# Turning a feed-forward's relu chunks to channels on VectorE and the transfer queue instead of TensorE

## The chip, the cores and the metric

The kernel runs on one core of a Trainium2 chip. The metric is device time in microseconds (us) of one execution. Engines are named as in the profile: PE is TensorE's matrix multiplication, PEld its weight loads, DVE is VectorE, ACT is ScalarE, POOL is GpSimd, SP is the SyncE queue that issues most transfers.

## The reference, cut to what matters

One decoder layer on 256 tokens of 2048 channels: a token mixer (pooling, gated spatial mixing, sparse attention, merged and projected), then a squared-relu feed-forward of width 8192. The part that the change touches is the feed-forward, with its surroundings:

```
h = rms_norm(x, norm_g[l, 2]) * (1.0 + scale2) + shift2
f = jnp.square(jax.nn.relu(h @ w_ff1[l])) @ w_ff2[l]
x = x + gate2 * rms_norm(f, norm_g[l, 3])
```

All inputs are float32. `w_ff1` is 2048 x 8192 and `w_ff2` 8192 x 2048.

## The kernel before, in words

Every product is made from three matmuls in the type fp32r: activation and weight are each split into a high part and a low part, and high x high, high x low and low x high are summed (lines 188 to 190). The activation is the stationary operand, with channels on the 128 partitions (`hhi`, `hlo` for the first feed-forward product, `fhi`, `flo` for the second); the weight streams, 512 columns at a time. The result therefore comes out with tokens on the partitions, and has to be turned before it can be the activation of the next product.

One `gemm` makes 512 output columns for both token tiles from 16 slices of 128 input channels (`kt`). It has four units. Each unit loads 1 MB of weights into one of three `raw` buffers (line 165, on SP), splits it in two halves (`whi` on ACT, line 175; `wlo` on DVE, line 176; three buffers each), and multiplies: 12 matmuls for each half. So a gemm is 96 matmuls. What waits in the list `later` is issued behind the first unit of the next gemm.

The feed-forward runs in four quarters (`qt`). In each, four gemms over `ff1` (m = 0 to 3) make 512 hidden channels each, and then four gemms over `ff2` (n = 0 to 3) multiply the quarter's 2048 hidden channels and add to `fsum`. Behind each `ff1` gemm, ACT takes the relu of the two PSUM banks into `r_t` (line 945), tokens on partitions. `to_channels` then turns the chunk: eight 128x128 transposes on PE into the two `x` banks (`transposed`, line 345), squares on ACT from PSUM (line 936), and the split into `fhi` (ACT, line 398) and `flo` (DVE, line 399). `to_channels` of chunk m fills slices 4m to 4m+3 of `fhi` and `flo`. The second feed-forward product reads them in rising order, so those of m = 3 are first read three quarters into the gemm n = 0.

During the first two quarters a 1 MB block of `w_adaT` is loaded once a gemm into the same `raw` ring (line 262) and reduced on DVE (line 263).

Each engine's queue runs in order. The order is written before the run by the framework's planner: an instruction takes its place at the time at which the planner believes its operands ready, and among ready ones the earlier in the program goes first; the splits are moved ahead by 150 places (`ahead=150`). Semaphores then make each instruction wait for its real operands. Transfers of a queue share eight completion counters in turn.

Of the kernel before, what the change touches and what calls it, by code (L numbers as in the profile page):

```python
# [7 lines left out]
F32 = mybir.dt.float32  # L8
F32R = mybir.dt.float32r
AF = mybir.ActivationFunctionType  # L10
# [3 lines left out]
P = 128  # L14
# [3 lines left out]
NT = S // P  # L18
# [38 lines left out]
def trunk_kernel(ctx: ExitStack, tc: tile.TileContext, consts, vecs, w_adaT, win_e, win_g, win_n, brp_v, brg_v, brn_v,  # L57
                 wout_v, ff1_v, ff2_v, x, c, pool_w, gmlp_ln_g,
                 gmlp_ln_b, gmlp_ws, gmlp_bs, cmp_w1, cmp_w2, cmp_b2, out):
    nc = tc.nc  # L60
    V, A, T, G = nc.vector, nc.scalar, nc.tensor, nc.gpsimd

    def sbuf(name, side="left", stack=None):
        es = ExitStack()
        p = es.enter_context(tc.tile_pool(name=name, bufs=1, side=side, reuse_waits="tile"))
        (stack or ctx).push(es)
        return p, es
# [17 lines left out]
    def flat(t):  # L85
        return t.rearrange("p j s -> p (j s)")

    def bank(tag):
        return psum["pool"].tile([P, 512], F32, name=f"ps_{tag}", tag=tag, bufs=psum["bufs"][tag])
# [120 lines left out]
    def drain(name):  # L210
        while side[name][0]:
            step(side[name][0])


    later = []

    def gemm(wv, c0, act, k_tiles=KT, row0=0):

        ps = [mm_bank(), mm_bank()]
        for u in range(0, k_tiles, 4):  # L220
            raw = load_raw(wv[c0, (row0 + u) // 4])
            for h in range(2):
                k0 = u + 2 * h
                hv, lv = split(raw[:, 2 * h:2 * h + 2])
                mm_a(ps, k0, k0 == 0, k0 + 2 == k_tiles, act, hv, lv)
            while later:
                later.pop(0)()
            fill()
        return ps

    def gemm_a_last(wv, c0, act, stores, row0=0, between=None, after=()):


        ps = [mm_bank(), mm_bank()]
        kept = []
        for u in range(0, KT, 4):
            raw = load_raw(wv[c0, (row0 + u) // 4])
            for h in range(2):
                k0 = u + 2 * h
                left = (KT - k0) // 2  # L240
                own = left <= len(stores) + 3
                with ExitStack() as es:
                    if k0 >= 4:
                        for ins in after:
                            es.enter_context(tc.issue_after(ins.ins))
                    hv, lv = split(raw[:, 2 * h:2 * h + 2],
                                   stores[len(stores) + 3 - left] if 3 < left and own else None)
                mm_a(ps, k0, k0 == 0, left == 1, act, hv, lv, toks=(0,) if own else range(NT))
                if own:
                    kept.append((k0, hv, lv))  # L250
        if between:
            between(ps)
        for k0, hv, lv in kept:
            mm_a(ps, k0, k0 == 0, k0 + 2 == KT, act, hv, lv, toks=(1,))
        return ps
# [84 lines left out]
    def transposed(src, k2):  # L340

        tb = bank("x")
        for k in range(2):
            for t in range(NT):
                T.transpose(tb[:, (k * NT + t) * P:(k * NT + t + 1) * P],  # L345
                            src[t][:, (k2 * 2 + k) * P:(k2 * 2 + k + 1) * P], ident)
        return tb
# [49 lines left out]
    def hi_lo(hi, lo, src):  # L397
        A.activation(hi, src, AF.Copy)  # L398
        V.tensor_sub(lo, src, hi.bitcast(F32))  # L399
# [360 lines left out]
    tb = bank("x")  # L760
# [159 lines left out]
    fl, _ = sbuf("ff")  # L920
# [9 lines left out]

    def to_channels(m, r_t):

        for k in range(2):
            tb = transposed([r_t[:, t] for t in range(NT)], k)
            r32 = flat(fl.tile([P, 2, S], F32, name="r32", tag="r32", bufs=3))
            A.activation(r32, tb, AF.Square)
            s = slice(4 * m + 2 * k, 4 * m + 2 * k + 2)
            hi_lo(flat(fhi[:, s]), flat(flo[:, s]), r32)

    for qt in range(4):  # L940
        for m in range(4):
            ps = gemm(ff1_v, qt * 4 + m, act) if qt or m else ps_first
            r_t = fl.tile([P, NT, 512], F32, name="r_t", tag="r_t", bufs=2)
            for t in range(NT):
                A.activation(r_t[:, t], ps[t], AF.Relu)  # L945
            later.append(lambda m=m, r_t=r_t: to_channels(m, r_t))
        if qt == 3:
            drain("ada")
        for n in range(4):
            if qt == 3 and n == 3:  # L950
                ps = gemm_a_last(ff2_v, n, (fhi, flo), [[flat(h[:, 4 * k:4 * k + 4]) for h in act] for k in range(4)],
                                 row0=qt * 16)
            else:
                ps = gemm(ff2_v, n, (fhi, flo), row0=qt * 16)
            ns = slice(n * 512, (n + 1) * 512)
            for t in range(NT):
                if qt == 0:
                    V.tensor_copy(fsum[:, t, ns], ps[t])
                else:
                    V.tensor_add(fsum[:, t, ns], fsum[:, t, ns], ps[t])  # L960
                if qt == 3:
                    jk = xp.tile([P, 512], F32, name="jk", tag="jk", bufs=2)
                    A.activation(jk, fsum[:, t, ns], AF.Square, accum_out=ssq3[:, t, n:n + 1])
                    fg[n, t] = fsum[:, t, ns]
                    if n == 3:
                        fg[n, t] = flat(fl.tile([P, 2, S], F32, name="r32", tag="r32", bufs=3))
                    V.tensor_mul(fg[n, t], fsum[:, t, ns], gg2[:, ns])
# [94 lines left out]
```

## Time and profile before

| | us |
|---|---|
| median of three runs | 1498.44 |
| the three runs | 1493.22, 1498.44, 1505.2 |
| the profiled execution, its own time | 1494.34 |
| its span, first to last instruction | 1492.6 |
| PE busy | 1430.4 (96%) |
| DVE busy | 1038.5 (70%) |
| ACT busy | 819.9 (55%) |

The profiled execution's own time is 1.7 us above its span and 4.1 us below the median of the runs. The feed-forward's gemms run from about 775 us of the span to 1483.8 us; the last 8.8 us are the final normalisation and the stores.

### The profile page before, as it was taken

What the parts mean: (1) busy time and instruction counts of PE and PEld (TensorE: products, weight loads), DVE (VectorE), ACT (ScalarE), POOL (GpSimd) and SP (SyncE); (2) the same over time, 40 slices, a digit from 0 to 9 for tenths busy, and PEclk for the clock granted to TensorE, in tenths of its full rate; (3) what the DMA queues carried; (4) which work ended last, traced back from release to release, by engine and by line L of the source; (5) the groups of instructions that cost most, each with busy time, mean ns of one, the idle gap of its engine ahead of it and who ended that gap; (6) DMA issues with size and microseconds to landing.
All of it is one profiled execution on the core that took longest, in us unless ns stands there. A gap on an engine that the chain in (4) does not pass through costs nothing.

```text
span 1492.6 us, 17091 instructions
## 1 busy us (share of the span) xinstructions
PE 1430.4 (96%) x6504; PEld 1167.9 (78%) x6504; DVE 1038.5 (70%) x1297; ACT 819.9 (55%) x1200; POOL 29.8 (2%) x33
## 2 busy tenths in 40 slices
PE   3999999999999999999999999999999999999997
PEld 2777787788777777787778888888888888888886
DVE  7988887768988887788785566565565555444555
ACT  4566666964678874454574543355434554345442
POOL 0000001002010000000000000000000000000000
PEclk9999999999999999999999999999999999999999
DMA  8989788647767567788845666666675455555553
GB/s 321 370 334 366 297 331 307 243 158 245 258 223 280 198 240 306 283 309 317 308 182 190 225 236 237 240 240 241 224 254 191 175 197 199 197 197 178 189 197 113
DMA packets 54098, 365.47 MB, mean 245 GB/s; under 512 B 6128, under 2 KB 6272, under 8 KB 13824
## 3 DMA queue, kind: packets, MB, share of 16 engines
q1 hardware_dynamic: 52704, 360.14, 66.7%
q0 software_dynamic: 1312, 4.23, 0.9%
q8 instruction: 51, 0.84, 0.2%
q14 instruction: 31, 0.25, 0.0%
HBM read 362.26 MB, written 2.10 MB: 244 GB/s over the span
## 4 chain that ended last, share of the span: by engine, by line
PE 83%; DVE 9%; DMA 4%; ACT 3%; issue 1%; SPq 0%; DVEq 0%; ACTq 0%
PE ps_mm L189 26%; PE ps_mm L190 26%; PE ps_mm L188 25%; DVE wlo L176 3%; DVE raw L263 2%; PE ps_x L345 1%; ACT whi L175 1%; DMA raw<-in_win_g_dram 1%; DMA raw<-in_w_out_dram 1%; PE ps_x L668 1%; DMA x_h<-in_x_dram 1%; PE ps_pv L660 1%; PE ps_pv L659 0%; DMA raw<-in_w_br_pool_dram 0%; DMA raw<-in_w_br_nsa_dram 0%
## 5 line engine op out<-in xcount | busy, mean ns | idle before, releaser
L176 DVE TENSOR_TENSOR wlo<-raw,whi 128x1024 fp32r<-128x1024 f32 x479 | 570.9, 1203 | 359.5 <-ACT whi L175 357.2
L175 ACT ACTIVATE whi<-raw 128x1024 fp32r<-128x1024 f32 x479 | 492.6, 1036 | 494.4 <-PE ps_mm L190 409.1
L189 PE MATMUL ps_mm<-wlo,hhi 128*128 128x512 f32 x1240 | 488.4, 394 | 12.8 <-DVE wlo L176 12.8
L188 PE MATMUL ps_mm<-whi,hhi 128*128 128x512 f32 x1240 | 482.8, 394 | 10.0 <-ACT hhi L317 5.5
L190 PE MATMUL ps_mm<-whi,hlo 128*128 128x512 f32 x1240 | 485.9, 392 | 0.0
L189 PEld LDWEIGHTS ps_mm<-wlo,hhi 128*128 128x128 f32 x1240 | 233.8, 189 | 68.4 <-DVE wlo L176 21.4
L188 PEld LDWEIGHTS ps_mm<-whi,hhi 128*128 128x128 f32 x1240 | 233.2, 188 | 60.4 <-ACT whi L175 6.8
L190 PEld LDWEIGHTS ps_mm<-whi,hlo 128*128 128x128 f32 x1240 | 233.7, 189 | 47.8 <-DVE hlo L318 0.4
L263 DVE CUSTOM_DVE_ANT_0 raw<-raw,sil 128x2048 f32<-128x2048 f32 x96 | 219.9, 2292 | 6.6 <-DMA raw<-in_w_adaT_dram 6.6
L188 PE MATMUL ps_mm<-whi,fhi 128*128 128x512 f32 x496 | 193.3, 390 | 0.0
L190 PE MATMUL ps_mm<-whi,flo 128*128 128x512 f32 x496 | 193.0, 389 | 0.0
L189 PE MATMUL ps_mm<-wlo,fhi 128*128 128x512 f32 x496 | 193.0, 389 | 0.0
L190 PEld LDWEIGHTS ps_mm<-whi,flo 128*128 128x128 f32 x496 | 93.1, 188 | 19.4
L189 PEld LDWEIGHTS ps_mm<-wlo,fhi 128*128 128x128 f32 x496 | 93.1, 188 | 19.3
L188 PEld LDWEIGHTS ps_mm<-whi,fhi 128*128 128x128 f32 x496 | 93.1, 188 | 19.2
L395 ACT ACTIVATE ps_mm<-part 128x512 f32<-128x512 f32 x40 | 23.5, 597 | 10.9 <-DVE part L384 7.9
L641 ACT ACTIVATE e<-e,m 128x128 f32<-128x128 f32 (+1 forms) x64 | 28.2, 443 | 0.7 <-DVE m L638 0.6
L945 ACT ACTIVATE r_t<-ps_mm 128x512 f32<-128x512 f32 x32 | 18.8, 588 | 14.7 <-PE ps_mm L190 14.7
L188 PE MATMUL ps_mm<-whi,qe 128*128 128x512 f32 x64 | 24.8, 392 | 1.0 <-ACT whi L175 1.0
L189 PE MATMUL ps_mm<-wlo,qe 128*128 128x512 f32 x64 | 25.3, 395 | 0.5 <-DVE wlo L176 0.5
L345 PE MATMUL ps_x<-cst,x_h 128*128 128x128 f32 x32 | 6.9, 376 | 19.2 <-DVE x_h L336 16.9
L399 DVE TENSOR_TENSOR flo<-r,fhi 128x512 fp32r<-128x512 f32 x32 | 20.7, 689 | 6.4 <-ACT fhi L398 6.4
(287 smaller groups left out, 1124.2 us busy)
## 6 DMA issues: line engine op xcount, KB each, us to landing
raw<-in_w_ff_dram SPq DMA_DIRECT2D x128, 1024.0 KB, 4.8
raw<-in_w_adaT_dram SPq DMA_DIRECT2D x96, 1024.0 KB, 5.8
raw<-in_win_g_dram SPq DMA_DIRECT2D x32, 1024.0 KB, 5.0
raw<-in_win_e_dram SPq DMA_DIRECT2D x24, 1024.0 KB, 6.0
raw<-in_win_e_dram SPq DMA_DIRECT2D x24, 768.0 KB, 6.1
raw<-in_w_out_dram SPq DMA_DIRECT2D x16, 1024.0 KB, 5.5
raw<-in_w_br_nsa_dram SPq DMA_DIRECT2D x8, 1024.0 KB, 5.9
raw<-in_win_e_dram SPq DMA_DIRECT2D x12, 512.0 KB, 5.9
```

Source lines behind the costliest of these rows:

```text
L175: A.activation(hv, v, AF.Copy)
L176: V.tensor_sub(lv, v, hv.bitcast(F32))
L188: T.matmul(outs[t], ahi[:, kt, ts_], hv[:, k, c0:c0 + n], start=f, stop=False, skip_group_check=True)
L189: T.matmul(outs[t], ahi[:, kt, ts_], lv[:, k, c0:c0 + n], start=False, stop=False, skip_group_check=True)
L190: T.matmul(outs[t], alo[:, kt, ts_], hv[:, k, c0:c0 + n], start=False, stop=l, skip_group_check=True)
L263: V.tensor_tensor_reduce(raw, raw, sil, 0.5, 0.0, ALU.mult, ALU.add, accum_out=col)
L345: T.transpose(tb[:, (k * NT + t) * P:(k * NT + t + 1) * P], src[t][:, (k2 * 2 + k) * P:(k2 * 2 + k + 1) * P], ident)
L395: A.activation(ps, early[e][0][:, b * 512:(b + 1) * 512], AF.Copy)
L399: V.tensor_sub(lo, src, hi.bitcast(F32))
L641: A.activation(e[:, br, 0:L], e[:, br, 0:L], AF.Exp, scale=-1.0, bias=m8[:, hh, br:br + 1], accum_out=s8[:, hh, br:br + 1])
L660: T.matmul(po, v, pl, start=False, stop=lst)
L945: A.activation(r_t[:, t], ps[t], AF.Relu)
```

## The change

The relu chunk is turned in two steps. VectorE transposes each 32x32 block of a token tile in place of its position (two instructions a chunk, into `tr`), with the blocks' columns regrouped so that the block column j stands outside. Then 16 transfers on SP move each of the four partition quarters q of `tr` to partition quarter j of `moved`: each takes 32 partitions, two runs of 512 bytes on each, 32 KB. ACT's square reads `moved` from SBUF instead of PSUM, with the blocks put back in order by its access pattern. `to_channels` is issued right behind the relu and no longer put on `later`. TensorE's eight transposes a chunk fall away.

```
     def to_channels(m, r_t):
+        tr = fl.tile([P, 4, NT, 4, 32], F32, name="tr")
+        for t in range(NT):
+            V.transpose(tr[:, :, t], r_t[:, t].rearrange("p (m j i) -> p j m i", m=4, j=4))
+        moved = fl.tile([P, NT, 4, 4, 32], F32, name="moved", tag="moved", bufs=2)
+        for q in range(4):
+            for j in range(4):
+                nc.sync.dma_start(moved[32 * j:32 * j + 32, :, q].rearrange("p t m i -> p t (m i)"),
+                                  tr[32 * q:32 * q + 32, j].rearrange("p t m i -> p t (m i)"))
+        mv = moved.rearrange("p t q m i -> p m (t q) i")
         for k in range(2):
-            tb = transposed([r_t[:, t] for t in range(NT)], k)
             r32 = flat(fl.tile([P, 2, S], F32, name="r32", tag="r32", bufs=3))
-            A.activation(r32, tb, AF.Square)
+            A.activation(r32.rearrange("p (m c i) -> p m c i", m=2, i=32), mv[:, 2 * k:2 * k + 2], AF.Square)
             s = slice(4 * m + 2 * k, 4 * m + 2 * k + 2)
             hi_lo(flat(fhi[:, s]), flat(flo[:, s]), r32)
...
-            later.append(lambda m=m, r_t=r_t: to_channels(m, r_t))
+            to_channels(m, r_t)
```

## Rows read from the trace of the kernel before

**Rows 1.** The page, part 1: busy time of each engine.
```profile
PE 1430.4 (96%) x6504; PEld 1167.9 (78%) x6504; DVE 1038.5 (70%) x1297; ACT 819.9 (55%) x1200; POOL 29.8 (2%) x33
```

**Rows 2.** Windows: length; PE, PEld, DVE, ACT, POOL busy; clock; DMA share.
```profile
820.66:843.32 22.66, 22.66 (x106) 18.85 (x105) 13.22 (x12) 11.58 (x14) 0.00 (x0) 1.00 0.65 233
...
866.00:975.70 109.70, 109.70 (x490) 90.91 (x489) 65.36 (x60) 45.55 (x46) 0.00 (x0) 1.00 0.69 240
...
1153.40:1176.60 23.20, 23.20 (x108) 19.25 (x107) 12.40 (x12) 12.58 (x16) 0.00 (x0) 1.00 0.52 182
...
1333.10:1355.80 22.70, 22.70 (x106) 18.87 (x105) 11.10 (x10) 11.58 (x14) 0.00 (x0) 1.00 0.53 185
```

**Rows 3.** Timeline of PE, one chunk's boundary and its transposes: start, duration.
```profile
815.21 0.39 PE L188 MATMUL ps_mm<-whi,hhi 128*128 128x512 f32 x1
...
820.43 0.40 PE L190 MATMUL ps_mm<-whi,hlo 128*128 128x512 f32 x1
820.66 1.03 PE L345 MATMUL ps_x<-cst,r_t 128*128 128x128 f32 x8
...
821.77 0.40 PE L189 MATMUL ps_mm<-wlo,hhi 128*128 128x512 f32 x1
```

**Rows 4.** Groups of 128x512 instructions from 785 us to 1483 us.
```profile
L399 DVE TENSOR_TENSOR flo<-r,fhi 128x512 fp32r<-128x512 f32 x32 | 20.7, 689 | 6.4 <-ACT fhi L398 6.4
...
L936 ACT ACTIVATE r<-ps_x 128x512 f32<-128x512 f32 x32 | 17.1, 585 | 0.0
...
L963 ACT ACTIVATE jk<-fsum 128x512 f32<-128x512 f32 x7 | 4.3, 618 | 9.0 <-DVE fsum L960 9.0
```

**Rows 5.** Timeline of ACT around the same boundary, with idle before.
```profile
814.73 0.60 ACT L945 ACTIVATE r_t<-ps_mm 128x512 f32<-128x512 f32 x1 [0.98 <-PE ps_mm L190]
815.41 1.06 ACT L175 ACTIVATE whi<-raw 128x1024 fp32r<-128x1024 f32 x1
816.38 0.58 ACT L945 ACTIVATE r_t<-ps_mm 128x512 f32<-128x512 f32 x1
818.13 1.06 ACT L175 ACTIVATE whi<-raw 128x1024 fp32r<-128x1024 f32 x1 [1.17 <-PE ps_mm L190]
...
832.63 1.06 ACT L175 ACTIVATE whi<-raw 128x1024 fp32r<-128x1024 f32 x1 [1.66 <-PE ps_mm L190]
```

**Rows 6.** Timeline of DVE around the same boundary.
```profile
814.93 2.28 DVE L263 CUSTOM_DVE_ANT_0 raw<-raw,sil 128x2048 f32<-128x2048 f32 x1
...
817.14 1.22 DVE L176 TENSOR_TENSOR wlo<-raw,whi 128x1024 fp32r<-128x1024 f32 x1
```

**Rows 7.** Timeline of SP there: weight loads issued.
```profile
815.04 0.33 SPq L165 DMA_DIRECT2D raw<-in_w_ff_dram  x1
...
817.25 3.56 SPq L165 DMA_DIRECT2D raw<-in_w_ff_dram  x2
```

**Rows 8.** Waits of the SP queue: total us, times, longest.
```profile
SPq L262 <- DMA x_h<-in_x_dram: 2.3, 2, 1.4
...
SPq L165 <- DMA sil<-in_c_dram: 0.7, 1, 0.7
```

**Rows 9.** Timeline of SP: issues of single transfers, first and last of the kernel.
```profile
1.18 0.42 SPq L129 DMA_DIRECT2D sil<-in_c_dram  x1
...
1488.80 0.33 SPq L974 DMA_DIRECT2D out_dram<-x  x1
```

**Rows 10.** DMA issues: count, size, median us from issue to landing.
```profile
raw<-in_w_ff_dram SPq DMA_DIRECT2D x128, 1024.0 KB, 4.8
...
out_dram<-x SPq DMA_DIRECT2D x8, 256.0 KB, 2.1
```

**Rows 11.** Waits of ACT from 785 us on.
```profile
ACT whi L175 <- PE ps_mm L190: 330.5, 219, 1.8
```

**Rows 12.** Waits of DVE from 785 us on.
```profile
DVE raw L263 <- DMA raw<-in_w_adaT_dram: 1.1, 1, 1.1
```

## The prediction

> **What bounds the kernel now.** I read the page's busy times first: PE is busy for 96% of the span [rows 1]. That is a mean, so I asked for the windows of the feed-forward, where the change lies. [...]
>
> **What is removed.** Eight transposes stand between two matmuls [rows 3]. Two matmuls on, without transposes, would be 2 x 0.227 = 0.45 us (96 matmuls in 21.76 us, below); with them it is 821.77 - 820.43 = 1.34 us, so they cost 0.89 us. The windows check it: a chunk with its transposes takes 22.66 us, and the window from 866.00 to 975.70 holds one such chunk and four gemms without, (109.70 - 22.66) / 4 = 21.76 us each [rows 2]; the difference is 0.90 us. The longer chunk of the third quarter, 23.2 us, holds two more 128x512 matmuls of another job (`to_rows`), which stay. Sixteen chunks give 16 x 0.90 = **14.4 us** off PE. It is the whole of the possible gain: 0.96% of 1494.3.
>
> **What is added, and what hides it.** I call T the first matmul of the gemm behind the chunk; in the rows T = 815.21 [rows 3].
>
> DVE gets two transposes of 128x512 a chunk. No row shows one. The nearest is a 128x512 TENSOR_TENSOR of 0.69 us [rows 4]; if four-byte elements need two passes it is nearer to the 128x1024 form, 1.22 us [rows 6]. Were it shorter than 0.69, nothing would be won, since DVE has room. I take 0.69, the same count of elements: 1.4 us a chunk (2.4 at the other end), beside 9.4 us of free time. Cost on the path: none, as long as `wlo` isn't late, which has 3.1 us in hand (worked out below). [...]
>
> When are they done? The second relu ends at 816.38 + 0.58 = T+1.75 [rows 5]. DVE is then in a reduction and next in `wlo`, until 817.14 + 1.22 = T+3.15 [rows 6]. The transposes end at T+4.5 (up to T+5.6).
>
> SP gets 16 transfers a chunk. An issue of one transfer takes 0.33 to 0.42 us [rows 9], so 16 take 5.3 to 6.7 us; for this form with two runs on each partition no row stands, and I bound it by the smaller row below and by twice that, 0.66 us, above. There is also a wait: early in the kernel loads wait for transfers that have nothing to do with their buffer (a `w_adaT` load for `x_h`, a weight load for `sil`) [rows 8], each for the transfer eight places before it in SP's order. So the ninth move waits for the first to land, and so on. A 256 KB store lands 2.1 us after its issue, a 1 MB load 4.8 us after [rows 10]; I bound a move's landing by these, since it may stand behind a load in flight. Eight issues take 2.6 to 3.4 us, so the counters add 0 to 2.2 us. Last issue: T+4.5+6+1 = T+11.5 (bounds T+10 to T+16); landing from T+13.6 to T+16.3 for that issue, middle T+15 (bounds T+12 to T+21).
>
> What is queued behind them on SP: the weight loads. The one issued at 817.25 + 3.56 - 0.33 = 820.48 = T+5.3 [rows 7] falls into the burst and goes behind it, to T+12 or T+13. It feeds the first unit of the gemm after next, whose `whi` runs at 832.63 [rows 5], 0.9 us earlier without transposes: T+16.5. The splits themselves are early: `whi` of a half is written when the half three before is done, two halves (2 x 2.72 us) before PE wants it, and needs 1.06 + 1.23 us, so 3.1 us are in hand. The load must land by T+19.6; issued at T+13 it lands at T+17.8. Hidden, with 1.8 us to spare. The next load finds its buffer at T+11.6, goes behind it and has the same slack. DMA load: 0.5 MB more beside 5 MB a chunk; were its 512-byte runs twice as dear, the share rises from 0.65 to about 0.78. Hidden.
>
> ACT: two squares a chunk from SBUF instead of PSUM, 0.62 us for 0.585 [rows 4]: nothing. But they now wait for the moves, and ACT's queue holds `whi` behind them. The planner's order is meant to put them where the moves land; it costs nothing as long as a square waits less than 3.1 us. The rows speak for the planner's estimate of landings being no shorter than the real one: the DVE reductions, which wait for 1 MB loads in the same way, waited once in this stage, 1.1 us [rows 12].
>
> **The four turns from ff1 to ff2.** There the chunk m = 3 is wanted three quarters into the next gemm, at T+16.3. The moves land at T+15, the square and `fhi` add 1.25 us and may find ACT in a `whi`: T+16.3 to T+17.3. So the margin that the transposes on PE had (they were done 6 us behind T) is used up. Stall: 0 to 5 us each, I take 1 us, 4 us in all, since the middle of the landing gives 0 to 1. In the other 12 chunks `fhi` is wanted at least a gemm later.
>
> **Sum.** 1494.3 - 14.4 + 4 = 1483.9 on the profiled execution. This one stood 4.1 us below the median of the runs; carried over, **1488**.
>
> [...] The rows show that transfers of one queue overlap: two weight loads were issued 2.2 us apart, each 4.8 us from issue to landing [rows 7, 10]. So I count the issue and not the landing of each move. [...]
>
> **Rivals.**
> *The square holds ACT* (slower). If the moves land later than the planner thinks by L, ACT stands at the square with `whi` behind it, and PE loses L - 3.1 us in each of 16 chunks. It eats the gain from L = 4.0 us on. At L = 5 us it is 16 x 1.9 = 30 us: 1498.4 - 14.4 + 30 = 1514. For it: the landing is uncertain by 4 us. Against it: rows 12. Chance 0.16.
> *The burst holds the loads.* If an issue with its counter waits takes 0.7 us instead of 0.45, the burst lasts 11.2 us, the load goes out at T+16 and lands at T+20.5: 0.9 us late, 16 x 0.9 = 14.4, just the gain: 1498. At 0.8 us: 1524. Chance 0.17, mostly on the near side.
> *The transfers don't overlap.* 16 x 2.1 = 33.6 us of queue in a chunk of 22.66 us: SP becomes the bound, with at least 16 x 11 us more, 1660 or above. Chance 0.03.
> That the transposes stay on PE is excluded by the diff.
>
> **How the numbers follow.** The forecast, with turns costing 0 to 2.5 us each, has 0.64 and covers 1484 to 1494 before the scatter of runs (1493 to 1505 for one kernel). A change of 1% is about what a measurement of this kernel can tell from none. The gain cannot pass 0.96%, so only scatter makes it faster by over 1%: 0.20 out of the 0.64. Same: the other 0.44, 0.14 of the second rival and 0.05 of the first. Slower: 0.11, 0.03 and 0.03. The range takes the full gain with a low run, 1494.3 - 14.4 - 1 = 1479, and the rivals' near sides, to 1506.
>
> **What would show it.** A chunk window of 21.8 us with PE busy throughout and no line 345 on `r_t`: the main step is right. DVE transposes near 0.69 us, moves issued every 0.33 to 0.45 us from about T+4.5, landing by T+16. PE idle before the matmul on `fhi` at the four turns: the third step. PE idle in every chunk, with ACT waiting on `moved`: the first rival; with `whi` waiting on `raw`: the second.

## The result and the profile after

| | before | changed |
|---|---|---|
| median, us | 1498.35 (5 runs, 1493.22 to 1505.2) | 1552.02 (5 runs, 1549.2 to 1554.37) |
| profiled execution, own time, us | 1494.34 | 1549.2 |

The ratio is 1.0382, with a 95% interval of 1.0356 to 1.0408. The forecast was 1488 with a range of 1479 to 1506: wrong in sign, and far outside the range.

The page's first part, of the changed kernel, against [rows 1]:

```profile
PE 1440.4 (93%) x6376; PEld 1166.3 (75%) x6376; DVE 1056.7 (68%) x1329; ACT 820.7 (53%) x1200; POOL 29.9 (2%) x33
```

PE has 128 instructions fewer and is busy for 10 us longer. Two things are therefore to be found: time in which PE stands still, and matmuls that take longer. The waits of PE and of ACT from 785 us to the end show the first (engine, tile and line, what it waited for; total us, times, longest):

```profile
PE ps_mm L188 <- ACT whi L175: 39.8, 10, 8.3
PE ps_mm L189 <- DVE wlo L176: 2.0, 4, 0.8
PE ps_mm L188 <- ACT fhi L398: 1.1, 1, 1.1
PE ps_mm L190 <- DVE flo L399: 0.6, 1, 0.6
```

```profile
ACT r L945 <- DMA moved<-tr: 64.3, 16, 10.3
ACT whi L175 <- DMA raw<-in_w_ff_dram: 27.1, 24, 2.2
```

The four sums of PE make 43.5 us, where PE had none in the windows of [rows 2]. ACT's two rows are two suspects: the square waits for the moves in all 16 chunks, with `whi` queued behind it (the first rival), and `whi` waits for weight loads (the second). By the sums the first is the larger, and that reading turns out to be wrong.

One chunk of the first quarter shows how a stall comes about. Its T, the first matmul of the gemm behind the chunk, is 843.57. SP's timeline (start, duration, operation, count):

```profile
843.39 0.33 SPq L165 DMA_DIRECT2D raw<-in_w_ff_dram  x1
846.74 10.86 SPq L940 DMA_DIRECT2D moved<-tr  x16
857.70 1.48 SPq L165 DMA_DIRECT2D raw<-in_w_ff_dram  x3
```

DVE's timeline in the same place, against [rows 6]:

```profile
843.73 0.71 DVE L936 STREAM_TRANSPOSE tr<-r_t 128x512 f32<-128x512 f32 x1 [0.37 <-ACT r_t L954]
...
846.01 0.71 DVE L936 STREAM_TRANSPOSE tr<-r_t 128x512 f32<-128x512 f32 x1
846.64 2.25 DVE L263 CUSTOM_DVE_ANT_0 raw<-raw,sil 128x2048 f32<-128x2048 f32 x1
```

The chain that ended last in the same stretch (start, duration, what):

```profile
857.70 5.00 DMA raw<-in_w_ff_dram
...
862.80 1.06 ACT whi L175
```

The `w_adaT` reduction used to start at T-0.3 and end at T+2.0 [rows 6]; the raw buffer that it gave back was loaded for the last unit of the next gemm at T+2.04 [rows 7]. The planner has now put both transposes and a `wlo` ahead of it. It ends at 848.89 = T+5.3, and by then SP is in its burst, which lasts 10.86 us. The load goes out at 857.70 = T+14.1 and lands at T+19.1. Its first matmul is the 73rd of the gemm, due at T + 72 x 0.227 = T+16.3; with 1.2 us for `whi` the load had to land by T+15.1. It is 4.0 us late. PE's timeline shows these 4 us, and what comes behind them:

```profile
859.67 0.39 PE L190 MATMUL ps_mm<-whi,hlo 128*128 128x512 f32 x1
863.91 1.22 PE L188 MATMUL ps_mm<-whi,hhi 128*128 128x512 f32 x2 [3.86 <-ACT whi L175]
...
866.20 0.63 PE L189 MATMUL ps_mm<-wlo,hhi 128*128 128x512 f32 x1
866.62 0.63 PE L190 MATMUL ps_mm<-whi,hlo 128*128 128x512 f32 x1
...
870.46 0.39 PE L190 MATMUL ps_mm<-whi,hlo 128*128 128x512 f32 x1
870.69 0.40 PE L188 MATMUL ps_mm<-whi,hhi 128*128 128x512 f32 x1
```

After the idle time the matmuls start every 0.43 us; from 870.46 on they start every 0.23 us again. The window between says why (the granted clock is the third figure from the end):

```profile
864.00:868.00 4.00, 3.96 (x9) 2.66 (x10) 3.48 (x3) 1.87 (x2) 0.00 (x0) 0.50 0.93 348
```

The clock is 0.50 here, where the windows of [rows 2] have 1.00. From 863.91 to 870.46 some 14 matmuls take 6.5 us instead of 14 x 0.227 = 3.2, a little of it a wait for `wlo`: this stall of 3.9 us costs about 7. The gemm before it, with a stall of the same length, takes 27.85 us; there the clock was 0.50 only from 836.3 to 839.7. The whole gemm of the rows, whose like took 21.76 us before [rows 2], takes 29.19:

```profile
843.57:872.76 29.19, 25.29 (x97) 19.84 (x96) 14.44 (x14) 11.66 (x15) 0.00 (x0) 0.88 0.56 198
```

This chunk is not like all others. In the first two quarters two weight loads stand between the `w_adaT` load and the burst in three chunks, one in three chunks (as above), and none in two. Behind two, PE waits for 0.8 us at most at a time; behind one for 3.2 to 3.9; behind none for 7.7 and 8.3. This is one of the two with none, T = 1009.27 (SP's timeline, and what SP waited for in it):

```profile
1011.94 10.62 SPq L940 DMA_DIRECT2D moved<-tr  x16
1022.65 1.48 SPq L165 DMA_DIRECT2D raw<-in_w_ff_dram  x3
```

```profile
SPq L940 <- DVE tr L936: 7.9, 1, 7.9
```

SP stood for 7.9 us at the head of the burst, waiting for the transposes. The raw buffer of the load behind it, which feeds the third unit of the next gemm, had been read for the last time at 1010.69 if the ring goes in turn; the load went out at 1022.65 all the same, and PE waited 8.3 us. Here it is the order of the queue, and not a late reduction, that holds the load.

The third quarter has no `w_adaT` load, but `to_rows` takes a ring buffer once a gemm. The load for the third unit goes out ahead of the burst, the others behind it. In a chunk with T = 1185.16:

```profile
1188.33 10.19 SPq L940 DMA_DIRECT2D moved<-tr  x16
1198.61 13.87 SPq L165 DMA_DIRECT2D raw<-in_w_ff_dram  x4
```

The first load behind the burst feeds the last unit of the next gemm. It went out at T+5.3 in the kernel before (1176.39, T = 1171.12) and goes out at T+13.5 now; it lands at T+18.6, and PE, which stopped at T+17.0, waits 2.8 us. All four chunks of the quarter do so. PE's waits are 11.6 us in the first quarter, 17.5 in the second, 12.7 in the third, and 1.7 at the last turn. The third quarter's row for `whi` (from 1184 to 1383 us):

```profile
PE ps_mm L188 <- ACT whi L175: 12.2, 4, 3.8
```

The fourth quarter has neither a `w_adaT` load nor `to_rows` in the ring. Its bursts are as long and stand at the same place of SP's order, and PE is busy throughout the gemms behind its first three chunks; one window of it:

```profile
1404.00:1428.00 24.00, 24.00 (x107) 19.79 (x107) 13.59 (x14) 12.88 (x17) 0.00 (x0) 1.00 0.63 220
```

So the moves alone do no harm, but for the last turn; moves and a ring with five users a gemm in three buffers do. The whole stage is measured from the first relu to the last (start of the first and the last in the row), 15 chunks and their gemms. Before, that is 609.2 us:

```profile
L945 ACT ACTIVATE r_t<-ps_mm x32: 577/581/599, 787.6 to 1396.8; 128x512 f32<-128x512 f32 x32
```

In the changed kernel it is 661.1:

```profile
L954 ACT ACTIVATE r_t<-ps_mm x32: 576/580/602, 789.1 to 1450.2; 128x512 f32<-128x512 f32 x32
```

### The profile page after: what moved, and what is told of

Its sections match the earlier page's. It is cut to its first block, busy times and chain, and to the rows that moved or that the text cites. A ratio compares the mean times of both kernels' runs of the same rounds, so it can differ in the third digit from the quotient of the medians.

```text
span 1547.4 us, 17244 instructions
## 1 busy us (share of the span) xinstructions
PE 1440.4 (93%) x6376; PEld 1166.3 (75%) x6376; DVE 1056.7 (68%) x1329; ACT 820.7 (53%) x1200; POOL 29.9 (2%) x33
## 4 chain that ended last, share of the span: by engine, by line
PE 70%; DVE 9%; SPq 8%; DMA 6%; ACT 4%; issue 2%; DVEq 0%; ACTq 0%
PE ps_mm L189 22%; PE ps_mm L190 22%; PE ps_mm L188 21%; SPq L940 8%; DMA raw<-in_w_ff_dram 4%; DVE wlo L176 4%; ACT whi L175 2%; DVE raw L263 1%; DVE tr L936 1%; PE ps_x L345 1%; PE ps_x L668 1%; DMA x_h<-in_x_dram 1%; PE ps_pv L660 0%; PE ps_pv L532 0%; PE ps_pv L659 0%
## 5 line engine op out<-in xcount | busy, mean ns | idle before, releaser
L188 PE MATMUL ps_mm<-whi,hhi 128*128 128x512 f32 x1240 | 487.9, 399 | 34.6 <-ACT whi L175 29.1
L189 PE MATMUL ps_mm<-wlo,hhi 128*128 128x512 f32 x1240 | 495.2, 399 | 11.5 <-DVE wlo L176 11.2
L189 PEld LDWEIGHTS ps_mm<-wlo,hhi 128*128 128x128 f32 x1240 | 237.6, 192 | 72.3 <-DVE wlo L176 23.8
L190 PEld LDWEIGHTS ps_mm<-whi,hlo 128*128 128x128 f32 x1240 | 237.4, 192 | 48.8 <-DVE hlo L318 0.4
L188 PE MATMUL ps_mm<-whi,fhi 128*128 128x512 f32 x496 | 194.8, 394 | 15.4 <-ACT whi L175 14.3
L945 ACT ACTIVATE r<-moved 128x512 f32<-128x512 f32 x32 | 18.4, 623 | 64.3 <-DMA moved<-tr 64.3
L384 DVE COPY part<-ps_mm 128x512 f32<-128x512 f32 x28 | 19.2, 687 | 10.0 <-PE ps_mm L190 10.0
```

The costliest lines, as they stand in the source:

```text
L188: T.matmul(outs[t], ahi[:, kt, ts_], hv[:, k, c0:c0 + n], start=f, stop=False, skip_group_check=True)
L189: T.matmul(outs[t], ahi[:, kt, ts_], lv[:, k, c0:c0 + n], start=False, stop=False, skip_group_check=True)
L190: T.matmul(outs[t], alo[:, kt, ts_], hv[:, k, c0:c0 + n], start=False, stop=l, skip_group_check=True)
L384: V.tensor_copy(d, ps)
L945: A.activation(r32.rearrange("p (m c i) -> p m c i", m=2, i=32), mv[:, 2 * k:2 * k + 2], AF.Square)
```

## The experiments

Two theories run through them. *The queue*: a burst of moves on SP holds a weight load that the ring of three buffers cannot wait for. *The square*: the squares that wait for their moves hold ACT, and `whi` with it. Later the first is split: is it the length of the burst, or its place in SP's order? In the expectations A is the theory of the queue; the others are named in each.

**e1, the kernel before with the moves added.** PE's transposes stay; the moves copy into a tile that nobody reads, so no square waits for them.

```
             later.append(lambda m=m, r_t=r_t: to_channels(m, r_t))
+            moved = fl.tile([P, NT, 4, 4, 32], F32, name="moved", tag="moved", bufs=2)
+            for q in range(4):
+                for j in range(4):
+                    nc.sync.dma_start(moved[32 * j:32 * j + 32, :, q]..., r_t[32 * q:32 * q + 32, :, 128 * j:128 * j + 128])
```

> The kernel before, with its transposes on PE, plus the 16 transfers a chunk on SP, copied from the relu tile into a buffer that nobody reads. Theory A (the burst on SP's in-order queue holds the next weight load): loads go out 10 us late though nothing waits for the moves, PE idles before matmuls whose weights are late, 1520 to 1550 us. Theory B (ACT stands at the square that waits for the moves, with weight splits behind it): nothing waits here, so 1498 to 1503 us.

Measured: 1519.98, ratio 1.0168 (1.0135 to 1.02). Waits of PE:

```profile
PE ps_mm L188 <- ACT whi L175: 10.4, 11, 1.6
```

The moves cost some 24 us where nothing waits for them. That leaves the queue, or the traffic of the moves itself; e6, below, has twice the bytes and hardly any of the loss. It isn't the whole loss: the change gives up 54 us against the kernel before, and 68 if the 14.4 that PE was relieved of are added. The bursts of e1 begin 1.4 us earlier than most of the change's, and none has all the loads behind it while a `w_adaT` block is in the ring.

**e2, the change without its moves.** The squares read `tr`, so the blocks of a chunk stay in their own partition quarter.

```
-        moved = fl.tile([P, NT, 4, 4, 32], F32, name="moved", tag="moved", bufs=2)
-        ...
-        mv = moved.rearrange("p t q m i -> p m (t q) i")
+        mv = tr.rearrange("p j t m i -> p m (j t) i")
```

> The changed kernel with the 16 transfers left out: the squares read the block-transposed tile itself, so that the channels are not gathered and the output is another one. A and B alike: all of the loss is gone and the 14.4 us of PE's transposes are won, 1484 us. Theory C (VectorE's transposes delay the splits or the reductions on DVE): 1490 us or more.

Measured: 1479.61, ratio 0.9895 (0.9862 to 0.9928), with no wait of PE in the stage. First to last relu takes 595.6 us, 13.6 less than before; the prediction's 15 x 0.90 is 13.5:

```profile
L949 ACT ACTIVATE r_t<-ps_mm x32: 578/580/602, 788.0 to 1383.6; 128x512 f32<-128x512 f32 x32
```

The gain is there in full, DVE's transposes cost nothing, and the whole loss lies with the moves.

**e3, the squares late.** The squares of m = 0 to 2 are queued on ACT behind the last split of the next gemm.

```
+        while at_end:
+            with tc.issue_after(last_whi[0].ins):
+                at_end.pop(0)()
...
+        if m < 3:
+            at_end.append(lambda: squares(m, mv))
+        else:
+            squares(m, mv)
```

> The changed kernel with the squares of m = 0 to 2 queued on ACT behind the last weight split of the next gemm, so that no split of that gemm stands behind a square. A: the load still goes out behind the burst, 1535 to 1552 us. B: the stalls of twelve of the sixteen chunks go, 1490 to 1505 us.

Measured: 1553.9, ratio 1.0391 (1.0348 to 1.0435). ACT's waits, against the two suspects above:

```profile
ACT whi L178 <- DMA raw<-in_w_ff_dram: 71.2, 20, 14.4
ACT r L958 <- DMA moved<-tr: 25.0, 9, 10.1
```

The square no longer stands in front, and `whi` waits for the same late loads under their own name. The 64.3 us of the changed kernel were a wait in parallel with a load that came later still. The theory of the square falls as the cause of the loss.

**e4, the moves on POOL's queue.** `nc.sync.dma_start` becomes `nc.gpsimd.dma_start` for all 16.

> The changed kernel with the moves issued on POOL's queue instead of SP's. A: the loads are no longer held, 1484 to 1500 us, as far as the moves land in time. B: the square still waits for the moves, and later ones if POOL issues more slowly, 1530 us or more.

Measured: 1538.66, ratio 1.0287 (1.025 to 1.0324). The loads are in time, but the moves are not. The row of the page's sixth part (KB each, median us to landing), and PE's largest waits:

```profile
moved<-tr POOLq DMA_DIRECT2D x256, 32.0 KB, 4.5
```

```profile
PE ps_mm L188 <- ACT fhi L398: 19.1, 4, 7.3
PE ps_mm L188 <- ACT whi L175: 9.4, 5, 3.5
```

From SP a move lands in 1.9 us (median), from POOL in 4.5 and up to 7.7. The square now does hold ACT, and the four turns from `ff1` to `ff2`, where `fhi` is wanted at once, cost up to 7.3 us each. So the first rival exists; on SP it was not what ended last.

**e5, a buffer of its own for the `w_adaT` blocks.** The ring then has four users a gemm, as in the fourth quarter (`to_rows` has its own too). For room `moved` and `r_t` have one buffer.

```
-            d32 = st.tile([P, 2048], F32, name="raw", tag="raw", bufs=3)[:, 0:512]
+            d32 = (small[0].tile([P, 512], F32, name="jk2", tag="jk2", bufs=2) if small else
+                   st.tile([P, 2048], F32, name="raw", tag="raw", bufs=3)[:, 0:512])
...
+    ring[:] = [fl, 1]
+    small.append(xp)
```

> The changed kernel with the fifth user of the weight ring taken out of it: in the feed-forward the w_adaT blocks get a buffer of their own, and the small tile of to_rows another pool's; moved and r_t have one buffer instead of two to make room. The 16 transfers stay on SP. Theory A1 (the burst holds a load only because five users share three buffers, which leaves a load no lead): the first three quarters run like the fourth, whose chunks showed no idle PE, 1484 to 1494 us. Theory A2 (a burst of 11 us is too long for any load): 1535 to 1552 us, as after the change.

Measured: 1512.28, ratio 1.0137 (1.0113 to 1.0161), with `PE <- whi` 14.3 us in five times, 11.4 of them in the first quarter. 36 of the 54 us are gone (each against the kernel before in its own rounds) with bursts as long as they were. In the first two quarters the loads' order changed with the buffer. In the third it did not: the order of SP's queue is that of the changed kernel and the bursts last 10.2 to 11.3 us, but PE's waits fall from 12.7 us to none. So the ring's lead decides what a burst costs. It is not the lead alone, or the rest would be gone too.

**e6 and e8, the moves by way of DRAM.** One store of `tr`, 512 KB, and four loads of 128 KB; in e8 also the buffer of e5.

```
+        nc.sync.dma_start(scr, tr.rearrange("p j t m i -> p j t (m i)"))
+        for j in range(4):
+            nc.sync.dma_start(moved[32 * j:32 * j + 32]..., scr[:, j].rearrange("(q r) t n -> r q (t n)", q=4))
```

> The changed kernel with the gathering done by five transfers instead of 16: one store of the block-transposed tile to DRAM and four loads, each of 32 partitions and 1 KB runs, after it; four squares of 256 columns instead of two of 512. A: five issues of 0.64 us hold SP for 3.2 us beside a wait of 2 to 3 us, the next load goes out by T+9.5 and lands by T+14.5, so little idle: 1484 to 1500 us. B (ACT at the square) or the extra traffic: 1520 us or more.

> Both mendings together: five transfers through DRAM, and the w_adaT blocks out of the weight ring. A: no load is late and no square holds ACT, so the gain of the transposes is left, less the turns: 1480 to 1488 us, faster than the kernel before by 0.6 to 1.0%. If the turns from ff1 to ff2 cost more than 1 us each: 1488 to 1500 us.

Measured: e6 1488.08, ratio 0.9959 (0.9943 to 0.9975); e8 1488.01, ratio 0.996 (0.9944 to 0.9975). The store is issued in 0.33 us and the four loads in 1.75, and PE waits 1.5 us in e6, 5.1 in e8. Twice the bytes, five issues instead of sixteen, and the change is faster than the kernel before. What costs is issuing, not moving. The buffer adds nothing here. First to last relu is 13.1 us shorter in e6, but the whole run only some 6: in its profiled run the stage began 5.5 us later. Starts of the first relu between 781 and 793 us occur in runs whose queue orders ahead of the stage are the same; why is open.

**e7, half of the moves.** Eight of the sixteen; POOL sets the rest of `moved` to zero.

```
+        G.memset(moved, 0.0)
-            for j in range(4):
+            for j in range(q % 2, 4, 2):
```

> The changed kernel with every second of the 16 transfers left out (8 a chunk; the other parts of the tile are zeros, so the output is another one). If the load's lead is a threshold (A): the burst takes 5.2 us, the load goes out at T+8.5 and lands at T+13.5, before T+14.2, and nearly all of the loss is gone: 1482 to 1494 us. If each transfer costs its share: half of the loss, (1480 + 1552) / 2 = 1516 us.

Measured: 1481.81, ratio 0.9938 (0.9917 to 0.996), PE waits 0.7 us. Half the moves cost nothing, rather than half. But the planner had also changed SP's order: in the first two quarters every burst has two weight loads ahead of it and two behind. Length and order had to be told apart. The third quarter does part them: SP's order there is the changed kernel's, with bursts of 5.1 to 6.1 us, and of PE's 12.7 us of waits 0.7 are left:

```profile
PE ps_mm L189 <- DVE wlo L176: 0.7, 2, 0.5
```

**e10, the reduction first.** The planner is told to place the `w_adaT` reduction earlier (`tc.high_priority(offset=300)` around it), so that its buffer comes free ahead of the burst.

> The changed kernel, all sixteen moves on SP; in the feed-forward the planner is told to place the w_adaT reduction ahead of the transposes, as it stood before the change. So the raw buffer comes free some 5 us earlier, and the load into it can be issued ahead of the burst. Theory A (what decides is which load stands behind the burst, and the reduction's place decides that): the stalls of the first two quarters become fewer, those of the third (no reduction there) stay: 1500 to 1530. Theory B (any burst of 10 us is too long for the ring whatever stands where): another load falls behind the burst instead, and the time stays within 1% of 1552.

Measured: 1547.03, ratio 1.037 (1.0357 to 1.0384): by the number the rival is right. The trace shows why: the order of the loads became uneven. SP's timeline of two neighbouring chunks:

```profile
818.11 4.74 SPq L165 DMA_DIRECT2D raw<-in_w_ff_dram  x2
824.27 10.18 SPq L944 DMA_DIRECT2D moved<-tr  x16
...
845.07 10.18 SPq L944 DMA_DIRECT2D moved<-tr  x16
855.35 8.85 SPq L165 DMA_DIRECT2D raw<-in_w_ff_dram  x4
```

Behind the burst with two loads ahead PE stood still for 1.9 us; behind the one with none ahead, for 6.9. Two bursts of one length, two prices, as in the changed kernel. The edit didn't set the order that it was meant to set, so the next run did so directly.

**e11, the order set.** All 16 moves on SP, each burst queued behind the load of the next gemm's last unit: two loads ahead, two behind.

```
             raw = load_raw(wv[c0, (row0 + u) // 4])
+            if u == k_tiles - 4 and due:
+                with tc.issue_after(last_load[0].ins):
+                    due.pop()()            # the moves, the squares and the split
```

> The changed kernel with all sixteen moves on SP, but each burst is queued behind the load of the last unit of the next gemm, so that two weight loads stand between the w_adaT load and the burst and two behind it, instead of one and three; this is the order that SP's queue has in the runs with eight moves, where TensorE hardly waited. The burst stays at 10 to 11 us. Theory A (what decides is which load stands behind the burst): the last unit's load goes out at about T+5.3, when the reduction has freed its buffer, and lands in time; the load behind the burst goes out at about T+16.5, lands at T+21.5, and is 2 us late at most: 1490 to 1515, some of it at the turns, where the moves now land at about T+18. Theory B (a burst of 10 us is too long for the ring in whatever order): 1540 or above.

Measured: 1520.03, ratio 1.0176 (1.0139 to 1.0212), 5 us above what A expected: 26 us are lost against the kernel before in its own rounds, where the changed kernel lost 54. SP around one burst, and PE's largest waits in the stage:

```profile
838.62 4.17 SPq L168 DMA_DIRECT2D raw<-in_w_ff_dram  x2
842.85 11.57 SPq L950 DMA_DIRECT2D moved<-tr  x16
854.51 1.00 SPq L168 DMA_DIRECT2D raw<-in_w_ff_dram  x2
```

```profile
PE ps_mm L191 <- ACT whi L178: 9.9, 6, 2.2
PE ps_mm L191 <- ACT fhi L404: 9.5, 4, 3.2
```

The late load is now the one behind the burst, which feeds the first unit of the gemm after next; it costs PE 2.2 us at most instead of 8.3. This is the order that the prediction assumed, and even so the change loses. The bursts not only last longer than it assumed, they also begin later: in the chunk shown at T+8.0, where it had T+4.5, since each now stands behind a load that waits for the reduction. At the turns the moves, now later, cost up to 3.2 us.

**e12, the burst shortened.** The four moves whose quarter stays the same (q = j) are copies on POOL's engine; twelve moves stay on SP. In the first two quarters one load is ahead in five chunks and two are in three.

```
+        for q in range(4):
+            G.tensor_copy(moved[32 * q:32 * q + 32, :, q], tr[32 * q:32 * q + 32, q])
         for q in range(4):
             for j in range(4):
+                if j == q:
+                    continue
```

> The changed kernel with the four moves that stay in their own partition quarter (q = j) made as copies on POOL, so that twelve moves are left on SP, in the same place of SP's order as the sixteen: one weight load ahead of the burst, three behind. The burst shrinks from 10.9 to about 7.7 us, and the load of the last unit goes out at about T+11 instead of T+14.1. Theory A (the load behind the burst must land by T+14.2 and lands 5 us after its issue): it is 1.8 us late instead of 5; TensorE's waits fall to a third, and less of the clock is lost: 1495 to 1515. Theory C (the order alone decides, the length doesn't matter): 1545 or above.

Measured: 1500.2, ratio 1.0049 (1.003 to 1.0067). PE's waits:

```profile
PE ps_mm L189 <- DVE wlo L176: 7.9, 13, 0.8
PE ps_mm L188 <- ACT whi L175: 5.4, 6, 1.7
```

With a burst of 7.6 to 8.7 us instead of 10.2 to 11.5 the loss against the kernel before falls from 54 us to 6, and the longest wait from 8.3 to 1.7 us. Part of that is order, since no burst of the first two quarters has no load ahead any more. In the third quarter the order is the changed kernel's, the bursts last 7.6 to 8.3 us, and PE's waits are 4.5 us instead of 12.7, nearly all in this row:

```profile
PE ps_mm L189 <- DVE wlo L176: 4.3, 8, 0.8
```

Length and order each count: at one order 10.2 to 11.3 us cost 12.7, 7.6 to 8.3 cost 4.5 and 5.1 to 6.1 cost 0.7; at one length the price goes by the loads ahead.

**e9 and e13, two queues.** In e9 eight moves are on SP (q < 2) and eight on POOL's queue. In e13 four are copies on POOL's engine as in e12, eight are on SP and four on POOL's queue:

```
+                (G if (j - q) % 4 == 2 else nc.sync).dma_start(...)
```

> The changed kernel with the sixteen moves shared out: eight on SP's queue (q = 0 and 1), eight on POOL's. Theory A (the burst on SP delays a weight load that the ring of three buffers gives no time to spare): the burst on SP falls from 10.9 to about 5 us, which the run with eight moves showed to be short enough; nothing is behind the moves on POOL. Then TensorE stands still only at the turns from ff1 to ff2, by what the moves on POOL land late (up to 5 us each in the run with all moves on POOL, with half of them about 2): 1482 to 1492. Theory B (small transfers are too slow each, wherever they are queued, and the square that waits for them holds ACT): the moves on POOL land in 4 to 5 us, the square waits as in the run on POOL, and half or more of the loss stays: 1510 or above.

> A version meant to beat both: the four moves with q = j are copies on POOL, eight moves stay on SP (two weight loads ahead of the burst, two behind), four are on POOL's queue. Theory A: the burst on SP is 5 us, the four on POOL are issued within 2.2 us and land by T+9 to T+11, so no square holds ACT: TensorE's waits under 2 us in all, 1478 to 1487. Theory B (whatever is queued on POOL lands too late): as in the run with eight on each queue, 1488 to 1494.

Measured: e9 1491.33, ratio 0.9987 (0.9972 to 1.0001); e13 **1480.64**, ratio **0.9916** (0.9897 to 0.9935). In e9 PE waits 4.9 us, the longest of 3.1 for a `whi`. In e13 the only wait is the first row; the second is PE's busy time and the clock from the first relu to the last, the third POOL's moves (compare 4.5 in e4), the last the relus, 596.8 us from first to last:

```profile
PE ps_mm L189 <- DVE wlo L176: 0.3, 1, 0.3
```

```profile
786.30:1383.10 596.80, 596.49 (x2629) 492.71 (x2628) 358.51 (x344) 283.75 (x320) 68.72 (x120) 1.00 0.65 228
```

```profile
moved<-tr POOLq DMA_DIRECT2D x64, 32.0 KB, 1.8
```

```profile
L958 ACT ACTIVATE r_t<-ps_mm x32: 578/580/602, 786.3 to 1383.1; 128x512 f32<-128x512 f32 x32
```

e13 computes all that the change computes and beats both kernels: 13.3 us below the kernel before in its own comparison, of 14.4 to be had. What was short is the issuing queue's time: in e13 a burst takes 5.1 to 5.8 us of SP a chunk instead of 10.2 to 11.5.

## Why the prediction was wrong

**The sum of what is removed was right.** In the windows of [rows 2] PE is busy throughout at a clock of 1.00, so its own work set the time there. 14.4 us was the forecast; e2 gives 13.6 from first to last relu, where 13.5 was due.

**DVE's transposes were right in size.** One takes 0.705 us where 0.69 was taken and 1.2 was the other end:

```profile
L936 DVE STREAM_TRANSPOSE tr<-r_t x32: 668/705/712, 789.8 to 1451.8; 128x512 f32<-128x512 f32 x32
```

The row shows that a transpose takes hardly longer than an elementwise instruction on as many elements (0.69 us), and nothing like the 1.22 us of the prediction's other end.

The transposes were to cost nothing "since DVE has room". DVE has (22.66 less 13.22, or 9.4 us, in the first chunk of [rows 2]); but the reduction behind them gives a raw buffer back, and in the chunk shown ends 3.3 us later. The prediction asked only whether `wlo` would be late.

**The issue of a move was mis-sized.** 0.33 to 0.42 us was taken, from transfers that go to or from DRAM, and 0.66 kept as a bound. The row:

```profile
L940 SPq DMA_DIRECT2D moved<-tr x256: 585/595/1462, 797.3 to 1462.1; - x128
```

0.595 us, one every 0.64, and 10.2 to 11.5 us for a burst instead of 7. The bounds held it, but the value was taken at the lower one. The landing, 1.9 us, lay just under the 2.1 of its lower bound, and T+15 for all moves is what came out (the square starts at 858.98 = T+15.4), since the burst began earlier and lasted longer.

**The step that failed is "What is queued behind them on SP".** It took one load, the one issued at T+5.3 before, as the load behind the burst, due by T+19.6 and "hidden, with 1.8 us to spare". It read this from one boundary of the first quarter and carried it to all sixteen chunks. The runs showed three things in its place:

- In three chunks of the first quarter the load for the last unit of the next gemm, issued at T+2.04 before [rows 7], fell behind the burst too, because its buffer came free later. In the chunk shown it was due at T+15.1 and landed at T+19.1; the three cost 11.6 us.
- In two chunks of the second quarter the load for the third unit, issued at T-0.2 before [rows 7], stood behind the burst as well. They cost 7.7 and 8.3 us.
- In the third quarter the load of T+5.3 is the one for the last unit of the next gemm, since `to_rows` shares the ring, and is wanted 3.8 us sooner than reckoned: to land by T+15.8 (PE stops at T+17.0, `whi` takes 1.2 us). Even the prediction's own T+17.8 would have been late. The four cost 12.7 us.

The mis-sized issue made each of these dearer, as the third quarter's 12.7, 4.5 and 0.7 us at one order show. Setting the order alone (e11, with later bursts) leaves 1520 us; the shorter burst in a partly better order (e12) leaves 1500; with neither it is 1552.

**The stalls were priced without the clock.** The rivals counted a late load at its lateness. From first to last relu the changed kernel needs 64.3 us more than e13, which has the same matmuls (661.1 against 596.8). Some 42 of them are PE's waits (43.5 less the 1.7 of the last turn, which comes after the last relu). The other 22 are busy time: the same 2629 matmuls keep PE busy for 619.0 us instead of e13's 596.5, at a mean granted clock of 0.96 instead of 1.00, as the row of e13 above and this one of the changed kernel show:

```profile
789.10:1450.20 661.10, 619.01 (x2629) 502.88 (x2628) 355.32 (x344) 283.69 (x319) 0.00 (x0) 0.96 0.59 208
```

In the stretches without a stall shown above the clock was 1.00; behind the stall shown it was 0.50.

**The turns** were taken at 1 us each. The single one that shows is the last, 1.1 us for `fhi` and 0.6 for `flo`; at the others a load was later.

**The rivals.** The second one, the burst that holds the loads, is what happened. Its price was 1498 at 0.7 us an issue and 1524 at 0.8. At the real 0.64 its working, with the prediction's order, would have given no loss at all, and e11 measured 1520: it counted one load by the first quarter's rows, with a burst from T+4.5, and left out the turns and the clock. The first rival, the square that holds ACT, exists, as e4 shows, but was hidden behind the loads (e3). [rows 12], taken as a sign that squares would hardly wait, misled: they waited in all 16 chunks, up to 10.3 us. The third, moves that don't overlap, did not happen: a move lands 1.9 us after its issue and the next is issued 0.64 us after it. The cost is the issuing queue's time rather than bandwidth, as e6 shows: twice the bytes, 0.33 and 1.75 us of issuing a chunk, and 1488.08 us.

**Open.** Why the planner puts one, two or no load ahead of a burst; whether the `w_adaT` reduction kept at its old place, with the order otherwise as it is, would have sufficed for the first quarter (e10 meant to try it and changed more; the third quarter has no reduction and stalls as well); and the start of the stage, which varies by several microseconds without a cause in the queues.

## What to carry to other kernels

An in-order queue that also carries the loads of a busy ring has a budget: the time between the moment a buffer comes free and the last moment at which its load may be issued. Compare a burst's whole issue time with the smallest such gap, for every load that may fall behind it and in every stage that uses the ring differently, and not for the one that one boundary showed before. An instruction added to an engine with time to spare can still delay the one behind it that gives a buffer back, by 3.3 us in the chunk shown. When two waits overlap, the larger sum need not be the cause: take its wait away by moving it (e3), and see whether the time moves.

## What the hardware showed that was not expected

- A transfer of 32 partitions with two runs of 512 bytes, SBUF to SBUF, takes SP 0.595 us to issue; a 1 MB load [rows 7] or a 512 KB store to DRAM takes 0.33.
- The same transfer takes 0.54 us on POOL, and lands in 4.5 us (median) when sixteen are queued there and in 1.8 when four are (e4, e13).
- After 3.9 us without a matmul PE ran at a granted clock of 0.50 and came back to 1.00 only 6.5 us after it had resumed. After another stall of 3.9 us it took 3.6 (changed kernel, 863.9 and 836.1 us).
